# RWKV time mixing on one core: numerators in two PSUM banks with one output operation, state matmuls in the denominators' banks, and every second v cast by GpSimd

## The chip, the core and the metric

The kernel runs on one core of a Trainium2 chip. A core has five engines, each with its own stream of instructions that it starts in order: TensorE (PE; its weight loads are listed as PEld), VectorE (DVE), ScalarE (ACT), GpSimd (POOL) and SyncE (SP). [...] The metric is device microseconds of one execution.

## The reference

Batch 16, 2048 time steps, 256 channels, float32. Channels and batches are independent, and time is a recurrence:

```
for b in range(batch):
    aa, bb, pp = 0, 0, -1e38
    for t in range(seq_len):
        kk, vv = k[b, t], v[b, t]
        ww = u + kk;  qq = max(pp, ww);  e1, e2 = exp(pp - qq), exp(ww - qq)
        output[b, t] = (e1 * aa + e2 * vv) / (e1 * bb + e2 + 1e-08)
        ww = pp - w + kk;  qq = max(ww, kk);  e1, e2 = exp(ww - qq), exp(kk - qq)
        aa, bb, pp = e1 * aa + e2 * vv, e1 * bb + e2, qq
```

So an output is a weighted sum of v over the past, divided by the sum of the weights. aa and bb are the two running sums, and pp is their scale.

## The kernel before

**Tiles.** Time is cut into 16 chunks of 128 steps, and each chunk into two halves of 64. A unit n = 4c + p is chunk c of four batches: 128 time steps on the partitions by 4 x 256 values (512 KB of k, 512 KB of v, 512 KB of output). There are 64 units. The text calls one pass of the main loop, line 342, a slot; slot n starts unit n, and an output follows nine or ten slots later.

**What one unit goes through.** `round_k` (L161) copies k to a matmul type. `logs` (L170, L174) makes the logarithms of two sets of weights, E and Z, in a four-bank PSUM tile X: triangular matrices times k, plus multiples of w and u. `exps` (L178, ACT) takes exponentials into EZR, a ring of 12 units with four parts: E, Z, E·v and Z·v. `times_v` (L196) writes the last two, from a bfloat16 copy of v. Nine slots later `den` (L296) sums E and Z into two PSUM banks, and `recip` (L302, L303) takes the reciprocal on ACT as a logarithm and an exponential. Ten slots later `num` (L309) sums E·v and Z·v for one half of the columns (i = 0 or 1) into one bank, `mult` (L316) multiplies by the reciprocal, both run again for the other half, and `store` (L321) writes the unit.

**PSUM.** Eight banks: X has four, `den` two, `num` one, and "misc" one, which the three state tiles tot, TS and CT share. Each pool has a single buffer, so a producer waits until the last reader of the tile before it has finished.

**v.** The even units, and those below 8, come as float32 and are cast by DVE (`cast_v`, L191). The odd ones from 9 on are cast on their way in by the transfer (L70).

**The state.** E and E·v sum only within a half. What comes in from earlier halves is carried by a small chain per chunk: `sums` (L218, 16 narrow matmuls), `copy_sums` (L225), `turn` (L232, 4 transposing float32 matmuls), `state_logs` (L237, ACT), `state_offsets` (L243 to L250, 7 DVE operations), `state_weights` (L254, ACT, tile G), `state_chain` (L261 to L268, 6 DVE operations, ending in CB), `turn_back` (L275), and `inject` (L280, L285). The last copies the result to cb, and four transfers on SP's queue put it in the last row of each half of E and E·v of the chunk's own four units. `den` and `num` then sum it with the rest, so `den(4c)` in slot 4c + 9 must wait for these transfers.

**What sets the order.** Every instruction is kept in program order, so the main loop is the order. In a slot it is: loads of unit n + 6, `exps(n)`, the state work named "pe0", "act" and "dve0", `num(n - 10)` first half, `den(n - 9)`, `recip`, `mult` first half, `num` second half, `logs(n + 1)`, `round_k(n + 2)`, `mult` second half, `store`, `times_v(n)`, `cast_v(n + 1)`, and the state work "pe" and "dve". The state work of chunk c is spread over four slots, which the text calls A to D:

```
slot          state work of chunk c, before
A  n = 4c+4   sums and copy_sums at the end
B  n = 4c+5   turn ahead of num; state_logs; state_offsets at the end
C  n = 4c+6   state_weights ahead of recip; state_chain at the end
D  n = 4c+7   turn_back and inject at the start
```

All large transfers (k, v and the outputs) are issued from POOL's queue, in program order with POOL's own work; those of `inject` are issued from SP.

Of the kernel before, what the change touches and what calls it, by code (L numbers as in the profile page):

```python
# [7 lines left out]
F32 = mybir.dt.float32  # L8
F32R = mybir.dt.float32r
BF16 = mybir.dt.bfloat16  # L10
ALU = mybir.AluOpType
ACT = mybir.ActivationFunctionType
# [3 lines left out]
def kernel(  # L16
# [9 lines left out]
    K = tc.keep_in_program_order  # L26
    PE, DVE, SC, POOL, SP = nc.tensor, nc.vector, nc.scalar, nc.gpsimd, nc.sync

    B, T, Dm = k.shape
    HS = 64  # L30
# [18 lines left out]
    psx = ctx.enter_context(tc.tile_pool(name="psx", bufs=1, space=bass.MemoryType.PSUM))  # L49
    psd = ctx.enter_context(tc.tile_pool(name="psd", bufs=1, space=bass.MemoryType.PSUM))  # L50
    psn = ctx.enter_context(tc.tile_pool(name="psn", bufs=1, space=bass.MemoryType.PSUM))
    psm = ctx.enter_context(tc.tile_pool(name="psm", bufs=1, space=bass.MemoryType.PSUM))

    K(SC.preload_act_table_set("natural_log_exp_and_others"))

# [1 line left out]
    kr_of, vr_of, VB = {}, {}, {}  # L57

    def v_mode(n):
        return "dve" if n < 8 or n % 2 == 0 else "dma"  # L60

    def load(n, kq=None, vq=None):
        c, p = divmod(n, 4)
# [29 lines left out]
    def select(ap, cmp, fill, base, cm, pattern):  # L93
        K(POOL.affine_select(out=ap, in_=ap, pattern=pattern, compare_op=cmp,
                             fill=fill, base=base, channel_multiplier=cm))
# [4 lines left out]
    def fill(ap, value):  # L100
        K(DVE.memset(ap.bitcast(F32) if ap.dtype == F32R else ap, value))
# [1 line left out]
    select(M1, GE, 0.0, -1, -1, [[1, 128]])  # L103
    select(I1, NE, 1.0, 0, -1, [[1, 128]])
    COf = matrix("COf", F32)
    for h in range(2):
        K(POOL.iota(COf[HS * h:HS * h + HS, :], pattern=[[0, 2], [1, HS]], base=-HS // 2 - h, channel_multiplier=0,
                    allow_small_or_imprecise_dtypes=True))
    for g in (2, 3):
        select(COf, NE, 1.0, -32 * g - 1, 1, [[0, 128]])  # L110
# [15 lines left out]
    mats = {}  # L126

    def sum_matrices():
        OH = consts.tile([128, 40], BF16, tag="OH", name="OH")
        fill(OH, 0.0)  # L130
        for h in range(2):
            fill(OH[HS * h:HS * h + HS, 8 + h:9 + h], 1.0)
            fill(OH[HS * h:HS * h + 1, 16 + h:17 + h], 1.0)
        Sel = consts.tile([128, 3, 2, 4, 2], F32, tag="Sel", name="Sel")
        fill(Sel, 0.0)
        for j, r in ((0, 64), (1, 0), (2, 8)):
            select(Sel[:, j], NE, 1.0, -r, 1, [[-1, 2], [-2, 4], [-32, 2]])
        mats["OH"], mats["Sel"] = OH, Sel.rearrange("p a h c i -> p (a h) (c i)")

    def out_matrices():  # L140
        Lx = matrix("Lx", F32)
# [14 lines left out]
    def ez(n):  # L156
        return EZR[:, :, n % RING]

    def round_k(n):
        km = consts.tile([128, 4, Dm], F32R, tag=f"km{n % 2}", name="km") if n < 2 else KM[n - 2]  # L160
        K(DVE.tensor_copy(km, kr_of.pop(n)))  # L161
        KM[n] = km
# [37 lines left out]
    LL = consts.tile([128, 2, 2 * NST + 2, 32], F32, tag="LL", name="LL")  # L200
    A_of = [consts.tile([128, 8, 32], F32, tag=f"A{j}", name=f"A{j}") for j in range(2)]
    AB_of = [consts.tile([128, 2, 2, 32], F32, tag=f"AB{j}", name=f"AB{j}") for j in range(2)]

    CB_of = [consts.tile([128, 4, 128], BF16, tag=f"CB{j}", name=f"CB{j}") for j in range(2)]

    def state_start():
# [4 lines left out]
        K(DVE.memset(AB_of[0][:, :, 0, :], 0.0))  # L211

    def sums(c):
        t = psm.tile([128, D], F32, tag="misc", name="tot")
        for p in range(4):
            for j in range(4):
                q, i = divmod(j, 2)
                K(PE.matmul(t[32 * j:32 * j + 32, :], mats["OH"][:, 8 - 2 * p:40 - 2 * p],  # L218
                            ez(4 * c + p)[:, 2 * q, i, :], start=p == 0, stop=p == 3,
                            tile_position=(0, 32 * j), skip_group_check=True))  # L220
        st[c, "tot"] = t

    def copy_sums(c):
        ts = tiny.tile([128, D], F32, tag="ts", name="ts")
        K(DVE.tensor_copy(ts, st.pop((c, "tot"))))  # L225
        st[c, "ts"] = ts

    def turn(c):
        TS = psm.tile([128, 6, 4, 8], F32, tag="misc", name="TS")
        ts = st.pop((c, "ts"))  # L230
        for b in range(4):
            K(PE.matmul(TS[:, :, b, :], ts[:, 128 * b:128 * b + 128], mats["Sel"], start=True, stop=True,  # L232
                        skip_group_check=True))
        st[c, "TS"] = TS.rearrange("p a b m -> p a (b m)")

    def state_logs(c):
        K(SC.activation(LL[:, :, 2 * c + 2:2 * c + 4, :],  # L237
                        st[c, "TS"][:, 2:6, :].rearrange("p (a h) x -> p a h x", a=2), ACT.Ln))

    def state_offsets(c):  # L240
        A, last = A_of[c % 2], A_of[(c + 1) % 2]
# [13 lines left out]
        st[c, "G"] = G  # L255

    def state_chain(c):
        G, TS = st.pop((c, "G")), st.pop((c, "TS"))
        AB, nxt = AB_of[c % 2], AB_of[(c + 1) % 2]
        tb = tiny.tile([128, 2, 2, 32], F32, tag="tb", name="tb")  # L260
        K(DVE.tensor_mul(tb, TS[:, 0:4, :].rearrange("p (a h) x -> p a h x", a=2),  # L261
                         G[:, 4:6, :].unsqueeze(1).broadcast_to([128, 2, 2, 32])))
        for h in range(2):
            x = tiny.tile([128, 2, 32], F32, tag="x", name="x")
            K(DVE.tensor_mul(x, AB[:, :, h, :], G[:, h, :].unsqueeze(1).broadcast_to([128, 2, 32])))
            K(DVE.tensor_add(AB[:, :, 1, :] if h == 0 else nxt[:, :, 0, :], x, tb[:, :, h, :]))
        CB = CB_of[c % 2]
        K(DVE.tensor_mul(bass.AP(tensor=CB.tensor, offset=CB.offset, ap=[list(CB.ap[0]), [64, 2], [32, 2], [129, 4], [4, 8]]),  # L268
                         AB.rearrange("p a h (b m) -> p a h b m", b=4),
                         G[:, 2:4, :].rearrange("p h (b m) -> p h b m", b=4).unsqueeze(1).broadcast_to([128, 2, 2, 4, 8])))  # L270

    def turn_back(c):
        CT = psm.tile([128, 128], F32, tag="misc", name="CT")
        for b in range(4):
            K(PE.matmul(CT, CB_of[c % 2][:, b, :], mats["Id"], start=b == 0, stop=b == 3, skip_group_check=True))  # L275
        st[c, "CT"] = CT

    def inject(c):
        cb = small.tile([128, 128], BF16, tag="cb", name="cb")
        K(DVE.tensor_copy(cb, st.pop((c, "CT"))))  # L280
        r0 = 4 * c % RING
        for q in range(2):
            for h in range(2):
                r, x = HS * h + HS - 1, 32 * (2 * q + h)
                K(SP.dma_start(  # L285
                    out=EZR[r:r + 1, 2 * (1 - q), r0:r0 + 4, :, :].rearrange("o p i (b x) -> o (p i b) x", b=4),
                    in_=cb[x:x + 32, :]))
# [15 lines left out]
        K(SC.activation(rd, rd, ACT.Exp, scale=-1.0))  # L303
        RD[n] = rd

    def num(n, i):
        d = psn.tile([128, D], F32, tag="num", name="num")
        for m, q in (("LN", 2), ("IdN", 3)):
            K(PE.matmul(d, mats[m], ez(n)[:, q, i, :], start=q == 2, stop=q == 3, skip_group_check=True))  # L309
        NUM[n, i] = d  # L310

    def mult(n, i):
        if i == 0:
            OT[n] = opool.tile([128, 4, Dm], F32, tag="ot", name="ot")
        o = OT[n].rearrange("p (i n) d -> p i (n d)", i=2)
        K(DVE.tensor_mul(o[:, i, :], NUM.pop((n, i)), RD[n][:, i, :]))  # L316

    def store(n):
        RD.pop(n)
        c, p = divmod(n, 4)  # L320
        K(POOL.dma_start(out=out[4 * p:4 * p + 4, c * TC:(c + 1) * TC, :].rearrange("n t d -> t n d"),  # L321
                         in_=OT.pop(n)))

    later = {}
    for c in range(NST):
        s = 4 * c + 3
        for slot, where, f in ((s + 1, "pe", sums), (s + 1, "dve", copy_sums),
                               (s + 2, "pe0", turn), (s + 2, "act", state_logs), (s + 2, "dve", state_offsets),
                               (s + 3, "act", state_weights), (s + 3, "dve", state_chain),
                               (s + 4, "pe0", turn_back), (s + 4, "dve0", inject)):  # L330
            later.setdefault((slot, where), []).append((f, c))

    def small_work(n, where):
        for f, c in later.pop((n, where), []):
            f(c)
# [6 lines left out]
    for n in range(NP + LAG + 2):  # L342
        q, qp = n - LAG, n - LAG - 1
        live, out_q, out_qp = n < NP, 0 <= q < NP, 0 <= qp < NP
        if n + AHEAD < NP:
            load(n + AHEAD)
        if live:
            exps(n)
        small_work(n, "pe0")
        small_work(n, "act")  # L350
        small_work(n, "dve0")
        if out_qp:
            num(qp, 0)
        if out_q:
            den(q)
            recip(q)
        if out_qp:
            mult(qp, 0)
            num(qp, 1)
        if n + 1 < NP:  # L360
            logs(n + 1)
        if n + 2 < NP:
            round_k(n + 2)
        if out_qp:
            mult(qp, 1)
            store(qp)
        if live:
            times_v(n)
        if n + 1 < NP:
            cast_v(n + 1)  # L370
        if n == 1:
            sum_matrices()
        if n == 3:
            out_matrices()
        small_work(n, "pe")
        small_work(n, "dve")
    assert not later


# [29 lines left out]
```

## Time and profile before

| what | value |
|---|---|
| three runs | 400.68, 403.47, 408.91 us; median 403.47 |
| profiled execution | 401.16 us, of it a span of 399.2 us from the first to the last instruction |
| busy time | PE 286.8, DVE 283.7, ACT 260.6, POOL 158.9 us |
| mean granted TensorE clock | 0.923 |
| moved by transfers | 94.15 MB, mean 236 GB/s |

The profile is of one execution. Its page gives the busy time of each engine, the span in 40 slices, the chain of work that ended last, and groups of instructions by line. Each group has its busy time, the mean of one instruction in ns, and the time that its engine sat idle before it. The trace behind it answers further questions: who waited for whom, the instructions in order of time, or the busy times in a stretch. The starts of `exps` (L178) mark the slots: those of units 12, 24, 25, 26, 27, 28, 60 and 63 are at 77.93, 144.70, 148.49, 154.62, 159.84, 165.46, 339.12 and 354.10 us. In the profile, "clock" is the TensorE clock that was granted, as a share of the full one.

### The profile page before, as it was taken

The page shows a single profiled execution, that of the slowest core. Times are in us where ns is not written, and L with a number is a line of the kernel's source. Part 1 is how long each engine was busy: PE and PEld are TensorE (multiplying, and loading weights), DVE is VectorE, ACT ScalarE, POOL GpSimd, SP SyncE. Part 2 cuts the span into 40 slices and gives each one's busy share as a digit, 9 for nine tenths or more (in the row PEclk, how much of TensorE's full clock was granted, in tenths as well). Part 3 has the DMA queues.
Part 4 walks back from the last instruction along what each step waited for, and adds up shares of the span by engine and source line. Part 5 has one row for each costly group of instructions (what it writes and reads, how often), then busy time and mean ns, then how long its engine had stood idle before and what let it go on. Part 6 is the DMA issues. An engine that isn't in the chain of part 4 may idle for free.

```text
span 399.2 us, 4440 instructions
## 1 busy us (share of the span) xinstructions
PE 286.8 (72%) x1449; PEld 133.9 (34%) x1472; DVE 283.7 (71%) x559; ACT 260.6 (65%) x225; POOL 158.9 (40%) x203
## 2 busy tenths in 40 slices
PE   0345769787868697777789686869777778957672
PEld 0122334343424334333334242433433333423220
DVE  1266665877787877878777878787787977776542
ACT  1134344975777877877758777777787775876472
POOL 7134322452545453535435454545353531012131
PEclk9999857996999889999969999988999996999896
DMA  7978975699899989999989899997999991333344
GB/s 245 349 248 193 316 202 136 174 284 257 264 254 296 273 204 282 261 279 281 287 237 287 264 295 250 302 275 208 280 262 286 268 285 56 105 109 138 122 165 158
DMA packets 43062, 94.15 MB, mean 236 GB/s; under 512 B 6160, under 2 KB 22560, under 8 KB 43040
## 3 DMA queue, kind: packets, MB, share of 16 engines
q0 software_dynamic: 37824, 91.24, 78.2%
q1 hardware_dynamic: 4144, 1.59, 1.7%
q10 hardware_dynamic: 1072, 1.06, 0.9%
q8 instruction: 11, 0.18, 0.2%
q14 instruction: 11, 0.09, 0.1%
HBM read 67.13 MB, written 33.55 MB: 252 GB/s over the span
## 4 chain that ended last, share of the span: by engine, by line
PE 34%; DVE 29%; issue 21%; DMA 7%; ACT 4%; POOL 3%; POOLq 0%; DVEq 0%
DVE EZR L196 10%; PE num L309 10%; PE X L174 7%; DVE ot L316 7%; PE den L296 6%; DMA kr<-in_k_dram 4%; PE tot L218 3%; ACT EZR L178 3%; PE TS L232 3%; POOL out_dram L321 3%; DVE vb L191 3%; PE X L170 3%; DVE ts L225 2%; DMA out_dram<-ot 1%; DMA vr<-in_v_dram 1%
## 5 line engine op out<-in xcount | busy, mean ns | idle before, releaser
L178 ACT ACTIVATE EZR<-X 128x2048 bf16<-128x2048 f32 x64 | 120.0, 1875 | 51.7 <-PE X L174 51.4
L321 POOL DMA_DIRECT2D out_dram<-ot x64 | 48.9, 763 | 196.5 <-DVE ot L316 192.6
L316 DVE TENSOR_TENSOR ot<-num,rd 128x512 f32<-128x512 f32 x128 | 88.3, 690 | 53.7 <-PE num L309 44.5
L302 ACT ACTIVATE rd<-den 128x1024 f32<-128x1024 f32 x64 | 65.2, 1019 | 51.3 <-PE den L296 51.3
L196 DVE TENSOR_TENSOR EZR<-EZR,vb 128x2048 bf16<-128x2048 bf16 x64 | 77.8, 1216 | 5.4 <-ACT EZR L178 5.3
L309 PE MATMUL num<-EZR,LN 128*128 128x512 bf16 x121 | 49.0, 405 | 35.2 <-DVE ot L316 34.6
L303 ACT ACTIVATE rd<-rd 128x1024 f32<-128x1024 f32 x64 | 67.9, 1061 | 2.0
L66 POOL DMA_DIRECT2D kr<-in_k_dram x62 | 55.7, 899 | 16.9 <-DVE km L161 14.8
L170 PE MATMUL X<-WU,CO 1*128 1x512 f32 (+1 forms) x256 | 36.1, 554 | 27.9 <-ACT EZR L178 15.1
L174 PE MATMUL X<-km,NLE 128*128 128x512 f32 x128 | 51.9, 489 | 3.3 <-DVE km L161 3.3
L161 DVE CAST km<-kr 128x1024 fp32r<-128x1024 f32 x64 | 44.0, 688 | 8.6 <-DMA kr<-in_k_dram 6.1
L309 PE MATMUL num<-EZR,IdN 128*128 128x512 bf16 x114 | 46.3, 406 | 0.4
L174 PE MATMUL X<-km,NLZ 128*128 128x512 f32 x128 | 45.5, 440 | 0.0
L296 PE MATMUL den<-EZR,Id 128*128 128x512 bf16 x128 | 40.9, 403 | 0.1
L296 PE MATMUL den<-EZR,L 128*128 128x512 bf16 x126 | 40.4, 403 | 0.7
L170 PEld LDWEIGHTS X<-WU,CO 1*128 1x128 f32 (+1 forms) x256 | 13.5, 202 | 58.3 <-ACT EZR L178 26.5
L74 POOL DMA_DIRECT2D vr<-in_v_dram x34 | 31.0, 912 | 2.4 <-DVE vb L191 2.4
L309 PEld LDWEIGHTS <-IdN 128*128 128x128 bf16 x128 | 13.1, 102 | 54.7 <-issue 54.7
L174 PEld LDWEIGHTS X<-km,NLZ 128*128 128x128 f32 x128 | 27.0, 211 | 6.9
L174 PEld LDWEIGHTS X<-km,NLE 128*128 128x128 f32 x128 | 21.0, 207 | 21.5 <-issue 17.2
L232 PE MATMUL TS<-Sel,ts 128*128 128x48 f32 x128 | 17.4, 279 | 12.9 <-DVE ts L225 12.9
L275 PE MATMUL CT<-Id,CB 128*128 128x128 bf16 x64 | 7.6, 254 | 25.8 <-DVE CB L268 25.8
(53 smaller groups left out, 214.2 us busy)
## 6 DMA issues: line engine op xcount, KB each, us to landing
out_dram<-ot POOLq DMA_DIRECT2D x64, 512.0 KB, 4.1
kr<-in_k_dram POOLq DMA_DIRECT2D x62, 512.0 KB, 6.2
vr<-in_v_dram POOLq DMA_DIRECT2D x34, 512.0 KB, 6.6
vb<-in_v_dram POOLq DMA_DIRECT2D x28, 256.0 KB, 7.2
kr<-in_k_dram SPq DMA_DIRECT2D x2, 512.0 KB, 14.3
vr<-in_v_dram ACTq DMA_DIRECT2D x2, 512.0 KB, 5.7
EZR<-cb SPq DMA_DIRECT2D x64, 8.0 KB, 4.8
wuf<-in_w_dram SPq DMA_DIRECT2D x4, 2.0 KB
```

What stands on the lines that cost most here:

```text
L66: K((kq or POOL).dma_start(out=kr, in_=src[0]))
L161: K(DVE.tensor_copy(km, kr_of.pop(n)))
L170: K(PE.matmul(X[:, q, i, :], CO[g:g + 1 + q, :], WU[g:g + 1 + q, :], start=True, stop=False, tile_position=(g, 0), skip_group_check=True))
L174: K(PE.matmul(X[:, q, i, :], m, km[:, i, :], start=False, stop=True, skip_group_check=True))
L178: K(SC.activation(ez(n)[:, 0:2], X_of.pop(n), ACT.Exp))
L196: K(DVE.tensor_mul(ez(n)[:, 2:4], ez(n)[:, 0:2], vb.unsqueeze(1).broadcast_to([128, 2, 2, D])))
L296: K(PE.matmul(d[:, i, :], mats[m], ez(n)[:, q, i, :], start=q == 0, stop=q == 1, skip_group_check=True))
L302: K(SC.activation(rd, DEN.pop(n), ACT.Ln, scale=RS))
L303: K(SC.activation(rd, rd, ACT.Exp, scale=-1.0))
L309: K(PE.matmul(d, mats[m], ez(n)[:, q, i, :], start=q == 2, stop=q == 3, skip_group_check=True))
L316: K(DVE.tensor_mul(o[:, i, :], NUM.pop((n, i)), RD[n][:, i, :]))
L321: K(POOL.dma_start(out=out[4 * p:4 * p + 4, c * TC:(c + 1) * TC, :].rearrange("n t d -> t n d"), in_=OT.pop(n)))
```

## The change

- `num` makes both halves of the columns at once, in a tile of two banks; `mult` is one 128x1024 operation.
- The "misc" bank is given up for that. tot, TS and CT are now made in `den`'s tile: they wait until `recip` has read the denominators of their slot, and the `den` after them waits until DVE has copied them out.
- `sums` makes 32 matmuls of 256 columns in place of 16 of 512, so tot has 256 columns. `turn` makes 2 matmuls in place of 4, with 96 columns in place of 48. TS is copied to SBUF by a new DVE operation, `copy_turned` (192 columns), which `state_logs` and `state_chain` then read.
- `state_chain` writes CB as its fourth operation, ahead of the two that only the next chunk needs.
- State work moves in the slots (the last part of the diff): `turn` and `turn_back` now come behind `logs`, `state_offsets` and `state_weights` into slot C, `state_chain` to the start of slot D, `inject` to the end of slot D.
- In a slot `den` now precedes `num`, and `cast_v(n + 1)` precedes `mult` and `times_v(n)`.
- All v come as float32, and POOL casts the odd units from 9 on.

```diff
     def v_mode(n):
-        return "dve" if n < 8 or n % 2 == 0 else "dma"
+        return "pool" if n >= 8 and n % 2 else "dve"
...
     def sums(c):
-        t = psm.tile([128, D], F32, tag="misc", name="tot")
+        t = psd.tile([128, 2, D], F32, tag="den", name="tot")
         for p in range(4):
-            for j in range(4):
-                q, i = divmod(j, 2)
-                K(PE.matmul(t[32 * j:32 * j + 32, :], mats["OH"][:, 8 - 2 * p:40 - 2 * p],
-                            ez(4 * c + p)[:, 2 * q, i, :], start=p == 0, stop=p == 3,
-                            tile_position=(0, 32 * j), skip_group_check=True))
+            for o in range(2):
+                x = 24 - 16 * o - 2 * p
+                for j in range(4):
+                    q, i = divmod(j, 2)
+                    K(PE.matmul(t[32 * j:32 * j + 32, 0, 0:Dm], mats["OH"][:, x:x + 32],
+                                ez(4 * c + p)[:, 2 * q, i, Dm * o:Dm * o + Dm],
+                                start=p == 0 and o == 0, stop=p == 3 and o == 1,
+                                tile_position=(0, 32 * j), skip_group_check=True))
...
+    def copy_turned(c):
+        T6 = small.tile([128, 6, 32], F32, tag="T6", name="T6")
+        K(DVE.tensor_copy(T6.rearrange("p a x -> p (a x)"), st.pop((c, "TS"))[:, 0, 0:192]))
+        st[c, "T6"] = T6
...
-    def num(n, i):
-        d = psn.tile([128, D], F32, tag="num", name="num")
+    def num(n):
+        d = psn.tile([128, 2, D], F32, tag="num", name="num")
         for m, q in (("LN", 2), ("IdN", 3)):
-            K(PE.matmul(d, mats[m], ez(n)[:, q, i, :], start=q == 2, stop=q == 3, skip_group_check=True))
-        NUM[n, i] = d
+            for i in range(2):
+                K(PE.matmul(d[:, i, :], mats[m], ez(n)[:, q, i, :], start=q == 2, stop=q == 3,
+                            skip_group_check=True))
+        NUM[n] = d
...
-        K(DVE.tensor_mul(o[:, i, :], NUM.pop((n, i)), RD[n][:, i, :]))
+        K(DVE.tensor_mul(OT[n].rearrange("p (i n) d -> p i (n d)", i=2), NUM.pop(n), RD.pop(n)))
...
-        for slot, where, f in ((s + 1, "pe", sums), (s + 1, "dve", copy_sums),
-                               (s + 2, "pe0", turn), (s + 2, "act", state_logs), (s + 2, "dve", state_offsets),
-                               (s + 3, "act", state_weights), (s + 3, "dve", state_chain),
-                               (s + 4, "pe0", turn_back), (s + 4, "dve0", inject)):
+        for slot, where, f in ((s + 1, "pe", sums), (s + 1, "last", copy_sums),
+                               (s + 2, "pe", turn), (s + 2, "last", copy_turned),
+                               (s + 3, "act", state_logs), (s + 3, "dve", state_offsets),
+                               (s + 3, "act2", state_weights),
+                               (s + 4, "dve0", state_chain), (s + 4, "pe", turn_back),
+                               (s + 4, "last", inject)):
```

The loop's order after the change, with s = 4c + 3 above: `exps`, "act", "dve0", `den`, `recip`, `num`, `logs`, `round_k`, `cast_v`, `mult`, `store`, "dve", `times_v`, "act2", "pe", "last".

## The prediction

> **What bounds the kernel now.** The page's busy times first: no engine is full.
>
> ```profile
> PE 286.8 (72%) x1449; PEld 133.9 (34%) x1472; DVE 283.7 (71%) x559; ACT 260.6 (65%) x225; POOL 158.9 (40%) x203
> ...
> PE 34%; DVE 29%; issue 21%; DMA 7%; ACT 4%; POOL 3%; POOLq 0%; DVEq 0%
> ```
>
> The chain that ended last passes between PE and DVE: hand-overs set the time. Next the busy times by chunk, cut at the start of each slot B (us; PE, PEld, DVE, ACT, POOL busy; clock; DMA share; GB/s):
>
> ```profile
> 148.49:169.30 20.81, 15.97 (x94) 7.66 (x92) 17.05 (x34) 16.21 (x15) 10.00 (x12) 1.00 0.97 276
> 169.30:190.32 21.02, 16.26 (x95) 7.73 (x96) 17.25 (x34) 16.23 (x16) 10.19 (x13) 1.00 0.97 277
> 190.32:213.30 22.98, 18.70 (x98) 8.43 (x100) 17.43 (x34) 16.18 (x15) 10.39 (x14) 0.85 0.90 255
> ```
>
> A chunk takes 20.9 at full clock, and about every third one 23.0, with the clock at half for 7 us. Units 12 to 60 are 12 chunks in 261.2, 21.8 each. Then the timeline of one chunk, for what ends each wait:
>
> ```profile
> 161.61 0.40 PE L275 MATMUL CT<-Id,CB 128*128 128x128 bf16 x4 [1.81 <-DVE CB L268]
> 162.04 0.29 DVE L280 CAST cb<-CT 128x128 bf16<-128x128 f32 x1 [0.49 <-PE CT L275]
> 162.37 2.40 SPq L285 DMA_DIRECT2D EZR<-cb  x4
> ...
> 165.46 1.88 ACT L178 ACTIVATE EZR<-X 128x2048 bf16<-128x2048 f32 x1
> ...
> 169.30 1.88 ACT L178 ACTIVATE EZR<-X 128x2048 bf16<-128x2048 f32 x1
> ...
> 170.30 0.69 DVE L225 COPY ts<-tot 128x512 f32<-128x512 f32 x1 [0.73 <-PE tot L218]
> ...
> 171.04 1.09 PE L232 MATMUL TS<-Sel,ts 128*128 128x48 f32 x8 [0.80 <-DVE ts L225]
> ...
> 172.66 0.69 DVE L316 TENSOR_TENSOR ot<-num,rd 128x512 f32<-128x512 f32 x1 [1.67 <-PE num L309]
> ...
> 175.60 1.88 ACT L178 ACTIVATE EZR<-X 128x2048 bf16<-128x2048 f32 x1
> ```
>
> Slot A (165.46) takes 3.84: ACT's own work (exps 1.77, Ln 1.05, Exp 1.02). Slots B, C, D take 6.30, 5.25 and 5.6, since state work stands ahead of `num` on PE. Two more answers matter below. The instructions of L285, the inject transfers, give their time to landing:
>
> ```profile
> DMA to landing us min/median/max: 1.8/4.8/5.9
> ```
>
> And the timeline, with the clock by microsecond, shows where the clock falls:
>
> ```profile
> 134.89 0.38 PE L309 MATMUL num<-EZR,LN 128*128 128x512 bf16 x1 [1.77 <-DVE ot L316]
> ```
>
> ```profile
> 138.00:139.00 1.00, 0.14 (x2) 0.15 (x3) 0.76 (x3) 1.00 (x1) 0.76 (x2) 0.50 1.00 373
> ```
>
> Behind a PE gap of 1.77 us it is at half from about 136.75 to 143.6, and that slot lasts 7.3 in place of 5.6.
>
> **The change, added up.** I follow the four queues round one chunk after the change. A step is from one start to the next, from this trace: `den` 0.86, its end seen by ACT 1.06 after its start; X 1.62; km and cast 0.60; times_v 1.13; a semaphore 0.05. A `mult` of 1024 columns is extrapolated from 690 ns at 512 and 220 ns at 64 (L265): 1.23, a step of 1.14, 0.08 less than two halves. `num` lets `mult` start 1.05 after it. tot's copy of 256 columns is 0.42 and T6's of 192 is 0.36, between L225 (691 ns, 512) and L280 (291 ns, 128).
>
> 1. DVE alone, from `mult` in slot C to cb at the end of D: mult 1.14, seven offsets 1.40, times_v 1.13, chain 1.45 (the row's 1.5), km 0.60, cast 0.60, mult 1.14, times_v 1.13, cb 0.29 = 8.9. The offsets now stand behind `mult`, and G waits for them; behind G on ACT is the next `exps`, behind that X. Slot C gets longer (6.1), slot D falls to ACT's 3.9.
> 2. `den` of slot A now waits for cb, as CT lies in its banks. Semaphore and den 0.92, num 0.86, X until sums 1.51, sums 1.10, tot's copy 0.42 = 4.8.
> 3. The next `den` waits for that copy: 0.92, num 1.05, mult 1.14, times_v 1.13, T6 0.36 = 4.6. TS (at most the row's 1.09, I take 0.65) runs beside mult and times_v.
> 4. `den` of slot C waits for T6: 0.92, num 1.05 = 2.0.
>
> Together 20.3 against 20.9 at full clock: two banks and shorter state work buy 0.6, and the three copies that `den` waits for take the rest back. Two things come on top.
>
> **Inject.** cb came early in slot D and now ends it, and `den(4c)` needs the third and fourth transfer. Before it started 10 us after cb; by step 2 it wants to 4.9 after. The four issues take 2.40, the fourth starts 1.84 after the first, and lands at the row's median 4.8 later: 6.7. So PE waits 1.8, with X and the next `exps` queued behind. From below, a landing of 1.8 (an idle tail) makes 3.6 and no wait; from above, 5.9 and 0.6 more for an issue make 8.3, a wait of 3.4. I take the median, since the store and loads of slot D are still issued just ahead of cb. Chunk: 22.1.
>
> **Clock.** PE's gaps become about 1.8 and 2.0 in slot D, and 1.8 at the inject wait; before they were 1.70 and 1.75, and one chunk in three lost 2.1. More chunks will. But half clock in slot A stretches the very den, num and X that run beside the transfers: 20.3 + 2.1 = 22.4, hardly more than 22.1. I take 22.3 as the mean.
>
> [...]
>
> **At nothing, with the cover.**
> - sums: 16 matmuls of 512 took 1.05, the array's rate for four column strips. 32 of 256 have the same columns, from 0 more to one issue each at the old pace, 32 x 0.053 = 1.7, so 0.85 more. The inject wait covers 1.8 of it; without that wait I count 0.3.
> - POOL's cast, 128x1024: POOL's nearest rows are 241 ns at 16 columns and 293 at 128, a line that gives 0.7, and 342 ns at 128 eight times is 2.7. I take 1.3. It runs after the store (0.76) and two loads (0.75 each, 1.12 to 1.21 beside a DVE cast), some 2.7 after a `mult`, while DVE waits for `num`. Only above 1.8 does it meet the offsets. Behind it on POOL stands the store alone, which waits for a later `mult`; the odd v now take float32 buffers that a cast freed a slot before. POOL has 10 of 21 us busy, and SP's queue holds nothing but the injects.
> - DMA: 5 to 25 us moved 344 GB/s of float32 loads at a share of 1.05, so 1.6 us a load; the tail's stores (149 GB/s at 0.43) cost 1.5. Four units cost 18.8 a chunk. Before the share was 0.97 x 20.9 = 20.3, so a casting load cost over 2: the traffic eases. At 22 it binds nothing, at 18.8 it would.
>
> [...]
>
> **Ends.** To unit 12 before: 77.9. Slot 5 took 5.44 against 4.77 around it, since turn stood ahead of X: 0.7 less, 77.2. From unit 64's slot (some 359.9) to the end: 39.3. The last plain slots took 2.89 each (377.08 to 391.54 in five). After, num 1.05, mult 1.23 and a semaphore make 2.33: 2.8 less. Slots 64 to 68 took 17, by the steps above 14: 33.5.
>
> **Sum.** 77.2 + 13 x 22.3 + 33.5 = 400.6 of span; the profiled execution has 2.0 around it: 402.6, say 403. Against its own 401.16 that is 0.4% more; the median shown is 403.47, 2.3 above the profiled run.
>
> **Rivals.**
> - *Faster.* The injects land within 5 us of cb, with the queues eased, and the clock falls no oftener: 20.3 + 0.3 + 0.7 = 21.3, so 77.2 + 276.9 + 33.5 + 2.0 = 390. For it: landings of 1.8 in the idle tail. Against: 4.4 to 5.9 wherever all three streams ran.
> - *Slower by the clock.* The gaps at cb and at the inject wait each halve it, at places where nothing covers: 22.1 + 2.1 = 24.2, 427. It decides where the lost clock falls in slots B and C, behind the inject wait. For it: three gaps of 1.8 in a chunk. Against: a stretched slot A closes the third.
> - *Slower by POOL.* The cast takes 2.7, as eight affine selects would, and the offsets wait 0.9 in each chunk: 22.3 + 0.9 = 23.2, 414. For it: affine selects are POOL's only like rows. Against: the line through the other two.
> - *The change does not do what it says.* The four state tiles could stay in the way as before; but `turn` and `turn_back` do come behind X in program order, so that is excluded, and the cost is only in the copies.
>
> **Chances.** No change, at 403, 0.42, with its own range 396 to 411 (21.8 to 22.9 a chunk). The faster rival 0.22. Slower by the clock 0.18, by POOL 0.10, both in part 0.08. A measurement of this kernel tells about 2% from no change (its runs spread by 2%), which is 395 to 411.5. So faster 0.22, same 0.42, slower 0.36. For 8 in 10 the range takes in most of the faster case and stops short of the full clock loss: 387 to 424.
>
> **What would show it.** Slots A, B, C, D near 5.5, 6.6, 6.1 and 3.9. `den` in slot B waiting on an EZR transfer for 1 to 2 us; if it waits only on ts, step 2 was the limit and the faster rival holds. G (L262) starting right behind the last offset, and exps right behind G. `mult` near 1.23 x 64, T6 0.36, POOL's cast 0.7 to 1.8 with no DVE wait on it. Chunks of 24 with clock below 0.85 would speak for the clock. Wrong would be above all a chunk below 20.3, which would mean that the queues overlap in a way that the steps don't have.

## The result, and the profile after

The changed kernel takes 432.37 us (median of four runs, 431.75 to 439.18), the kernel before 402.14 (four runs, 400.68 to 408.91). The ratio is 1.074, with a 95% interval of 1.067 to 1.081. The forecast was 403, within 387 to 424: the kernel is slower, and beyond the range. The profiled execution has a span of 429.7.

The page's busy times, and its row of the granted clock in 40 slices of the span:

```profile
PE 302.8 (70%) x1634; PEld 147.5 (34%) x1664; DVE 284.5 (66%) x511; ACT 259.5 (60%) x225; POOL 185.8 (43%) x234
...
PEclk9999666697988959696878969696877889596888
```

DVE and ACT do as much as before, POOL 27 us more (the casts), and PE 16 us more, though its work hardly grew: its matmuls ran longer (one of `num` took 631 ns at 201 us, where the clock is at half, and 379 at 209, where it is full), and the clock is below 9 in 26 of the 40 slices, where it was in 12 before. The same chunks by windows, now cut where slot A starts; columns as before:

```profile
149.67:173.78 24.11, 18.78 (x103) 9.28 (x104) 17.39 (x31) 16.07 (x16) 11.86 (x14) 0.78 0.84 267
173.78:196.99 23.21, 17.29 (x105) 8.39 (x105) 17.59 (x31) 16.08 (x16) 12.20 (x14) 0.86 0.85 273
196.99:221.52 24.53, 18.76 (x102) 9.22 (x104) 17.38 (x31) 16.06 (x15) 11.86 (x14) 0.78 0.80 258
```

Not every third chunk is disturbed but every one, at a clock of 0.78 to 0.86 (0.78 to 0.87 over the twelve from unit 12 to 60). DMA is less busy than before (share 0.80 to 0.85, where it was 0.90 to 0.97). The timeline from the end of slot D into slot B; L284 is `turn_back`, L290 and L295 are `inject`, L306 is `den`:

```profile
195.12 0.50 PE L170 MATMUL X<-WU,CO 1*128 1x512 f32 x4 [1.64 <-ACT EZR L178]
...
196.58 0.40 PE L284 MATMUL CT<-Id,CB 128*128 128x128 bf16 x4
196.99 1.86 ACT L178 ACTIVATE EZR<-X 128x2048 bf16<-128x2048 f32 x1
...
198.81 0.28 DVE L290 CAST cb<-CT 128x128 bf16<-128x128 f32 x1
199.12 2.87 SPq L295 DMA_DIRECT2D EZR<-cb  x4
199.14 0.58 PE L306 MATMUL den<-EZR,L 128*128 128x512 bf16 x1 [2.16 <-DVE cb L290]
...
205.48 1.88 ACT L178 ACTIVATE EZR<-X 128x2048 bf16<-128x2048 f32 x1 [2.32 <-PE X L174]
207.32 0.42 DVE L227 COPY ts<-tot 128x256 f32<-128x256 f32 x1 [2.16 <-PE tot L219]
208.19 0.59 PE L306 MATMUL den<-EZR,L 128*128 128x512 bf16 x2 [0.92 <-DMA EZR<-cb]
```

PE is idle for 1.64 us ahead of X, and after 1.9 us of work for 2.16 more, until cb has been copied out of `den`'s banks. The clock by microsecond shows what follows (us, then the five engines, clock, DMA share, GB/s; the rows between 199 and 207 are left out, all at 0.50):

```profile
197.00:198.00 1.00, 0.00 (x0) 0.00 (x0) 1.00 (x2) 1.00 (x2) 0.00 (x0) 0.63 0.89 336
198.00:199.00 1.00, 0.00 (x0) 0.00 (x0) 1.00 (x2) 0.84 (x1) 0.95 (x2) 0.50 0.70 258
...
207.00:208.00 1.00, 0.27 (x8) 0.00 (x0) 0.68 (x2) 0.36 (x1) 0.00 (x0) 0.75 0.74 132
```

From 197.26 to 207.50 it is at half: 10.2 us, all of slot A but its first 0.3 and the first 2 us of slot B, though PE is busy nearly throughout from 200 to 207. Slot A lasts 8.49 here. Behind it, in slot B, `den` still waits 0.92 for the inject transfers, 9.1 after cb.

Two things about the clock are easily missed. First, the 35 times at which it changes in this trace, from 47.08 to 425.96, lie whole multiples of 3.41 us apart, and so do the 15 in the kernel before, from 47.78 to 392.52: here it falls at 197.26, rises at 207.50, falls at 221.16 and rises at 227.99, which is three, four and two such intervals. Each chunk loses the clock for two or three of them, 6.8 or 10.2 us. Second, it fell 0.28 into the gap of 2.16, so that most of that gap came too late to call it. The interval that ended with the fall is this window:

```profile
193.85:197.26 3.41, 1.86 (x12) 1.15 (x13) 3.31 (x10) 3.38 (x4) 0.19 (x1) 1.00 0.99 322
```

PE was busy for 1.86 of 3.41, a share of 0.55. From unit 12 to 60 that share is 0.52 to 0.55 in each of the 12 intervals that end with a fall, and 0.61 or more in the 43 others at full clock. In the kernel before the share does not part them: five intervals of 0.48 to 0.54 ended with a fall, and four of 0.48 to 0.53 did not.

The inject transfers' time to landing, and the two kinds of wait of `den` in the whole span (us, times, longest):

```profile
DMA to landing us min/median/max: 2.1/5.5/6.8
```

```profile
PE den L306 <- DVE cb L290: 27.7, 15, 2.2
PE den L306 <- DMA EZR<-cb: 14.6, 9, 2.7
```

The span is 30.5 longer than before. Units 12 to 60 take 285.4, 23.78 a chunk, where they took 261.2: 24.2 of it. After unit 60 follow 65.4 (before 60.1), and ahead of unit 12 are 78.9 (77.9).

### The profile page after: what moved, and what is told of

It reads as the page before. It is cut to its first block, busy times and chain, and to the rows that moved or that the text cites. A ratio compares the mean times of both kernels' runs of the same rounds, so it can differ in the third digit from the quotient of the medians.

```text
span 429.7 us, 4779 instructions
## 1 busy us (share of the span) xinstructions
PE 302.8 (70%) x1634; PEld 147.5 (34%) x1664; DVE 284.5 (66%) x511; ACT 259.5 (60%) x225; POOL 185.8 (43%) x234
## 3 DMA queue, kind: packets, MB, share of 16 engines
q10 hardware_dynamic: 1072, 1.06, 0.8%
## 5 line engine op out<-in xcount | busy, mean ns | idle before, releaser
L326 DVE TENSOR_TENSOR ot<-num,rd 128x1024 f32<-128x1024 f32 x64 | 78.3, 1223 | 85.1 <-ACT rd L312 50.0
L312 ACT ACTIVATE rd<-den 128x1024 f32<-128x1024 f32 x64 | 65.4, 1022 | 68.8 <-PE den L306 45.4
L306 PE MATMUL den<-EZR,L 128*128 128x512 bf16 x113 | 39.2, 419 | 58.9 <-DVE cb L290 27.7
L161 DVE CAST km<-kr 128x1024 fp32r<-128x1024 f32 x64 | 57.4, 898 | 6.7 <-DMA kr<-in_k_dram 4.2
L65 POOL DMA_DIRECT2D kr<-in_k_dram x62 | 52.0, 839 | 10.5 <-DVE km L161 8.3
L73 POOL DMA_DIRECT2D vr<-in_v_dram x62 | 48.5, 782 | 18.6 <-DVE vb L191 17.2
L174 PE MATMUL X<-km,NLE 128*128 128x512 f32 x128 | 54.8, 515 | 1.4 <-DVE km L161 1.4
L174 PE MATMUL X<-km,NLZ 128*128 128x512 f32 x128 | 48.3, 464 | 0.0
L320 PE MATMUL num<-EZR,LN 128*128 128x512 bf16 x127 | 44.7, 438 | 2.8 <-DVE ot L326 1.9
L306 PE MATMUL den<-EZR,Id 128*128 128x512 bf16 x114 | 43.1, 456 | 3.0 <-issue 2.9
L306 PEld LDWEIGHTS <-L 128*128 128x128 bf16 x128 | 11.6, 105 | 74.5 <-issue 57.1
L189 POOL CAST vb<-vr 128x1024 bf16<-128x1024 f32 x28 | 33.3, 1190 | 0.0
L191 DVE CAST vb<-vr 128x1024 bf16<-128x1024 f32 x36 | 26.5, 736 | 0.9 <-DMA vr<-in_v_dram 0.9
```

The costliest lines, as they stand in the source:

```text
L65: K((kq or POOL).dma_start(out=kr, in_=src[0]))
L174: K(PE.matmul(X[:, q, i, :], m, km[:, i, :], start=False, stop=True, skip_group_check=True))
L306: K(PE.matmul(d[:, i, :], mats[m], ez(n)[:, q, i, :], start=q == 0, stop=q == 1, skip_group_check=True))
L312: K(SC.activation(rd, DEN.pop(n), ACT.Ln, scale=RS))
L320: K(PE.matmul(d[:, i, :], mats[m], ez(n)[:, q, i, :], start=q == 2, stop=q == 3, skip_group_check=True))
L326: K(DVE.tensor_mul(OT[n].rearrange("p (i n) d -> p i (n d)", i=2), NUM.pop(n), RD.pop(n)))
```

## The experiments

The theory from these lines: two things late in each chunk lie side by side. One is the half clock that comes with PE's gaps around X and CT; the other is that `den(4c)` needs transfers which start only at the end of slot D. The rivals are POOL's cast, one of the two alone, and the issue of the 32 small matmuls of `sums`. The last falls by the trace: they took 1.06 us at full clock (lag10_ctfill), where 16 of twice the size took 1.05, and 1.9 at half.

The times beside the runs of the kernel before on the same chip (medians 403 to 405), and from each trace the clock and the mean chunk from unit 12 to 60 with its slots. Where the ratio is left out, the executions spread too widely to give one, and the slots of fill_swap and fill_den are those of executions of 422.68 and 438.86, longer than their medians:

| kernel | us (lowest to highest) | ratio to before, 95% | clock | chunk | A | B | C | D |
|---|---|---|---|---|---|---|---|---|
| before | 402.14 (400.68 to 408.91) | | 0.923 | 21.77 | 3.82 | 6.25 | 5.39 | 6.31 |
| the change | 432.37 (431.75 to 439.18) | 1.067 to 1.081 | 0.829 | 23.78 | 7.88 | 6.00 | 6.08 | 3.82 |
| lag10 | 423.74 (422.65 to 427.51) | 1.044 to 1.058 | 0.840 | 23.54 | 8.08 | 5.61 | 6.08 | 3.78 |
| fill | 457.91 (455.91 to 463.10) | 1.126 to 1.139 | 0.862 | 26.24 | 5.76 | 10.14 | 6.57 | 3.77 |
| lag10_fill | 381.07 (380.14 to 382.35) | 0.940 to 0.950 | 0.993 | 20.44 | 5.62 | 4.96 | 6.08 | 3.77 |
| lag10_ctfill | 382.70 (382.53, 382.86) | 0.936 to 0.956 | 0.985 | 20.46 | 5.65 | 4.97 | 6.07 | 3.77 |
| fill_ab | 437.17 (433.58, 440.75) | | 0.982 | 23.84 | 5.65 | 8.33 | 6.08 | 3.77 |
| fill_swap | 419.29 (415.90, 422.68) | | 0.936 | 23.43 | 5.76 | 7.71 | 6.19 | 3.77 |
| fill_den | 434.37 (423.37 to 441.72) | | 0.958 | 24.76 | 5.66 | 9.12 | 6.22 | 3.77 |
| dma_cast | 430.41 (429.49 to 432.65) | 1.061 to 1.072 | 0.816 | 23.87 | 8.21 | 5.81 | 6.08 | 3.77 |
| lag10_fill_dma | 382.24 (380.67 to 383.65) | 0.941 to 0.956 | 0.982 | 20.48 | 5.65 | 4.97 | 6.08 | 3.77 |
| before_fill | 390.86 (389.47 to 392.73) | 0.962 to 0.981 | 0.995 | 21.00 | 3.82 | 6.29 | 5.24 | 5.64 |
| before_pool | 428.53 (424.99 to 433.85) | 1.046 to 1.067 | 0.868 | 23.51 | 4.11 | 6.23 | 5.14 | 8.03 |
| before_pool_ahead | 432.28 (431.28 to 432.38) | 1.064 to 1.083 | 0.894 | 24.00 | 3.78 | 6.66 | 8.12 | 5.44 |
| early_lag10 | 391.75 (390.74 to 391.89) | 0.961 to 0.974 | 0.887 | 21.29 | 6.15 | 5.28 | 6.08 | 3.77 |
| early_fill | 367.12 (364.67 to 370.01) | 0.897 to 0.914 | 0.989 | 19.59 | 4.50 | 5.25 | 6.07 | 3.77 |

"Idle matmuls" below multiply an identity by an old unit's E into a place that the next matmuls overwrite or that nobody reads. They leave the outputs as they are and only keep PE at work while it would wait.

### lag10: the transfers get a slot more

```diff
-    LAG = 9
+    LAG = 10
```

> After the change, with denominators ten and numerators eleven slots after their unit (LAG 10), so that den(4c) has one more slot before it needs the inject transfers; one more slot at the end costs 2.4. Side by side (my theory: in slots A and B the half clock and the inject transfers run beside each other, and each hides most of the other): den in slot B no longer waits for a transfer, the 0.8 to 1.7 of it in over half of the chunks go, half clock stays: 13 x 0.7 less, 2.4 more, about 426. Clock alone: the transfers never bound, 435. Inject alone: the chunk falls from 23.8 to 20.5, about 392.

`den` never waits for a transfer in slot B any more, yet slot A is still at half clock (8.08) and the chunk gains 0.24 only. Between the two profiled executions (spans of 429.7 and 423.0), 5.9 are gained ahead of unit 12 and 2.9 in the chunks, and 2.0 lost behind unit 60. So the transfers alone are not the cause.

### fill: no long gap on PE in slots D and A

```diff
+        # ahead of CT's four matmuls, in CT's second bank
+        for i in range(7):
+            K(PE.matmul(t[:, 1, :], mats["Id"], ez(4 * c + 3)[:, 1, i % 2, :], start=True, stop=True, ...))
...
+        # ahead of num in slot D, in num's banks
+            for i in range(8):
+                K(PE.matmul(d[:, i % 2, :], mats["Id"], ez(n)[:, 1, i % 2, :], start=True, stop=True, ...))
```

> After the change, with idle matmuls whose results are overwritten or never read: 7 of 512 columns ahead of the four of CT, 8 ahead of num in slot D, so that PE has no gap over 1.5 us there. The clock should stay at full in slot A. Side by side: then den in slot B waits for the injects, which landed 7.7 to 9.1 after cb, and the chunk is 15.4 + 8 = 23.4: 427 and a clock above 0.93. Clock alone: 2.9 less in each chunk, 395. Inject alone: no change, 432.

A clear miss: 25.5 us slower. Slot A is at full clock, 5.76, as meant. But `den` in slot B now stands before transfers that have not landed:

```profile
214.60 1.86 ACT L178 ACTIVATE EZR<-X 128x2048 bf16<-128x2048 f32 x1
...
220.25 1.88 ACT L178 ACTIVATE EZR<-X 128x2048 bf16<-128x2048 f32 x1 [0.30 <-PE X L174]
224.47 0.59 PE L309 MATMUL den<-EZR,L 128*128 128x512 bf16 x1 [3.27 <-DMA EZR<-cb]
229.36 1.88 ACT L178 ACTIVATE EZR<-X 128x2048 bf16<-128x2048 f32 x1 [0.87 <-PE X L174]
```

Slot A is 5.65 (214.60 to 220.25) and slot B 9.11. `den` waits 3.27, and over that gap the clock falls, so that the next matmuls run at half: two of `num` take 1.06 here, 0.59 in slot A, and in most chunks those of X are slower too (two take 1.22 in place of 0.73). Slot A's half clock had been hiding most of this wait.

### lag10_fill: both

The edits of lag10 and fill together.

> Both edits, the later denominators and the idle matmuls. Side by side: neither is left, the chunk is the 20.3 of the steps, 13 x 3.4 less than 432 and 2.4 more: about 391, far more than the two edits alone add up to. Clock alone: as the idle matmuls alone, and 2.4. Inject alone: as LAG 10 alone.

```profile
174.40:194.86 20.46, 18.32 (x119) 9.42 (x119) 16.86 (x31) 16.08 (x16) 11.66 (x14) 1.00 0.93 308
```

One edit brings 8.6, the other costs 25.5, both together bring 51.3 (432.37 to 381.07), ten more than expected. Of the profiled span 40 are gained in the twelve chunks, 6.6 ahead of them and 5.2 behind. The two delays are largely parallel: without the waits for transfers the chunk is still 23.54, and without the half clock in slot A it is 26.24, since the late `den` then calls a half clock of its own in slot B. Without both the chunk is 20.44.

### lag10_ctfill: idle matmuls behind X alone

lag10 with the seven idle matmuls ahead of CT alone.

> LAG 10 and only the 7 idle matmuls ahead of CT. If the gap behind CT alone calls the half clock: 381 and a clock of 0.99 as with all idle matmuls. If the gap of 1.6 ahead of X does it too in some chunks, as gaps of 1.77 did in one chunk of three before: 388 to 400.

The chunk is 20.46. The wait ahead of X stays (1.62), the gap behind CT shrinks to 0.64, and the clock holds: work in this one place is enough. That does not make the length of the gap behind CT the cause: in early_lag10 below it is 1.02, and the clock still falls. The intervals of 3.41 here have PE busy for 0.59 or more of them, above the 0.52 to 0.55 at the falls of the change. But a chunk of 20.46 is almost six intervals (20.48), so they cut each chunk of this run at the same place; whether the clock would hold with the wait of 1.62 at another place is not shown.

### fill_ab, fill_swap, fill_den: the price of the transfers

fill_ab adds 14 idle matmuls behind `sums` in tot's second bank; fill_swap issues E·v's two transfers ahead of E's; fill_den puts ten idle matmuls into `den`'s banks ahead of `den(4c)`. All three include fill.

```diff
+        for i in range(14):                       # fill_ab, at the end of sums
+            K(PE.matmul(t[:, 1, :], mats["Id"], ez(4 * c + 3)[:, 1, i % 2, :], start=True, stop=True, ...))
...
-        for q in range(2):                        # fill_swap, in inject
+        for q in (1, 0):
...
+        if n % 4 == 0 and 8 <= n + LAG < NP:      # fill_den, in den
+            for i in range(10):
+                K(PE.matmul(d[:, i % 2, :], mats["Id"], ez(n)[:, 1, i % 2, :], start=True, stop=True, ...))
```

> After the change, with the idle matmuls of the run before and 14 more behind sums, in the bank of tot's tile that is not used, so that PE has work while den in slot B waits for the injects. LAG is 9 as in the change, so the inject wait stays and only the clock is cured. My theory after the first four runs: the inject wait by itself costs 3 a chunk at full clock (den starts 7.7 or more after cb, the chunk is 15.4 + 8 = 23.4), and the rest of the 458 is the half clock that this wait calls in slot B: 420 to 430, clock above 0.95. Rival: idle matmuls themselves slow the transfers or the chain: 450 or more.

The clock holds (0.982), but tot's copy waits for the idle matmuls too, and `den` comes when they end, 8.1 to 8.2 after cb in ten of the twelve chunks: they set slot B's 8.33 themselves. The run tells only that a `den` so late gives the time of the change at full clock as well.

> After the change, with the idle matmuls in slot D, and the four inject transfers issued in the other order, so that den waits for the first and second in place of the third and fourth. If what makes them late is the issue on SP's queue (2.6 to 3.0 for four), den starts 1.2 to 1.5 earlier in each chunk: 458 less 16 to 20, 440. If they land together once the bulk traffic ahead of them is through, the order changes nothing: 458.

From cb to `den` it took 5.0 to 8.2 (mean 6.6), against 7.0 to 8.5 in fill (7.8). That is 1.2 earlier, about two issues of 0.6, as the first of the two cases had it; the scatter is too wide to call the issue shown. The time fell by 39, twice what was expected, as five of the twelve chunks kept the clock at 1.00 (none in fill).

> The changed kernel with the idle matmuls of fill and ten more ahead of den of unit 4c (slot B), 2.1 us at full clock, written where den then writes; outputs unchanged. If the inject wait by itself costs 2.8 a chunk (7.9 from cb to den in fill, against 5.0 where nothing has to land): slot B 7.8, chunk 23.2, 12 chunks 279, with 80 ahead and 60 behind 419, and 2 around it, about 420, at a clock above 0.95. If the prediction's 1.8 were right, the idle matmuls themselves would set slot B at 7.1: chunk 22.5, 412. If the clock still halves in B, 440 or more.

The transfers landed later than in fill, so that `den` came 7.4 to 10.0 after cb, and the runs scatter from 423 to 442. Nine of the twelve chunks kept the clock, and took 22.90 to 24.83. Two of them (windows of one chunk each):

```profile
230.94:255.03 24.09, 20.88 (x131) 10.33 (x129) 17.61 (x31) 16.09 (x15) 11.95 (x14) 1.00 0.81 266
255.03:278.34 23.31, 20.91 (x131) 10.33 (x129) 17.60 (x31) 16.07 (x15) 11.97 (x14) 1.00 0.82 272
```

At a clock of 1.00 they took 24.09 and 23.31, with `den` 8.6 and 7.8 after cb. The nine lie 2.5 to 4.4 above lag10_fill's 20.44: that is the wait for the transfers by itself, 1.8 in the forecast. In the two shortest `den` came only 0.1 behind the idle matmuls, which bound them from below. The expected 420 was missed by 14: the landing varies more than I assumed, and three chunks lost the clock (27.4 to 28.0).

### dma_cast and lag10_fill_dma: the odd v cast by the transfer again

```diff
-        return "pool" if n >= 8 and n % 2 else "dve"
+        return "dve" if n < 8 or n % 2 == 0 else "dma"
```

The cast v lie in buffers of their own, and v's pool has four buffers in place of six.

> After the change, but the odd v from 9 on are cast by their transfer as before, in buffers of their own. If POOL's cast costs nothing on the path (side by side, and both others): 432, within 1%. If it is part of the loss, by a longer DVE cast beside it (km took 1.73 in place of 0.68 in slot C): up to 1.0 a chunk, 419.

> The changed kernel with LAG 10 and the idle matmuls, but odd v cast by the transfer. With clock and injects out of the way, this prices POOL's cast. If it is hidden: 381 within 1%. If the km cast beside it (1.74 in place of 0.69) costs on the path: up to 1 a chunk less, 368. If casting transfers load the DMA (20.3 a chunk by the sum on record against a chunk of 20.5): 385 to 390.

430.41 against 432.37, and 382.24 against 381.07: no cost of the cast shows in the change, at either clock. It takes 1.19 in the mean, and `mult` and the offsets do not wait for it. One operation is stretched beside POOL, `round_k`. Of the change's own timeline, first POOL's rows and then DVE's:

```profile
188.63 0.75 POOL L73 DMA_DIRECT2D vr<-in_v_dram  x1
189.37 1.41 POOL L189 CAST vb<-vr 128x1024 bf16<-128x1024 f32 x1
```

```profile
188.16 1.73 DVE L161 CAST km<-kr 128x1024 fp32r<-128x1024 f32 x1
190.28 1.23 DVE L326 TENSOR_TENSOR ot<-num,rd 128x1024 f32<-128x1024 f32 x1 [0.38 <-issue]
```

It takes 1.73 in place of 0.68, but `mult` behind it starts only when `num` is ready, 0.38 after km's end: slot C, where this is, has that room.

### before_fill: does the kernel before lose to the clock too?

Five idle matmuls ahead of `den` in slot C and five ahead of CT in slot D of the kernel before.

> The kernel before the change, with idle matmuls in its two PE gaps: 5 ahead of den in slot C and 5 ahead of CT's in slot D. If the clock is what the before kernel loses too, its chunks all take 20.9 to 21.2 in place of 21.8: 393 to 397, and the 381 of the changed kernel with both cures shows what the change itself brings at full clock (0.4 to 0.6 a chunk, and 6 at the end). If the gaps are not what halves its clock: 402 or more.

390.86, chunk 21.00: the forecast's 20.9 at full clock. The kernel before loses 11 to 14 us to half clock (402.14 above, 404.96 beside this run). With both at full clock, the change (lag10_fill) is ahead by 9.8 us: 0.56 in each chunk, and the rest at the two ends, where LAG 10 has its part too.

### before_pool and before_pool_ahead: the cast alone, in the order of before

```diff
-        return "dve" if n < 8 or n % 2 == 0 else "dma"
+        return "pool" if n >= 8 and n % 2 else "dve"
...
+        if n + 1 < NP and v_mode(n + 1) == "pool":    # before_pool_ahead alone: ahead of the first mult
+            cast_v(n + 1)                             # and of the store, in place of behind them
```

> The kernel before with only the odd v loaded as float32 and cast by POOL: this part of the change alone. Hidden cast: 403, the same. If the longer km cast beside it (1.74) meets the chain: up to 1 a chunk, 416. If the lighter DMA traffic helps: 395.

428.53: a miss by far, and slot D is 8.03 where it was 6.31. There the cast runs behind the store, and meets `state_chain`. In its timeline, L189 is the cast, L265 makes the chain's two products, and L275 is CT:

```profile
190.75 1.05 POOL L189 CAST vb<-vr 128x1024 bf16<-128x1024 f32 x1
...
190.95 0.94 DVE L265 TENSOR_TENSOR x<-AB,G 128x64 f32<-128x64 f32 x1
...
192.18 0.22 DVE L265 TENSOR_TENSOR x<-AB,G 128x64 f32<-128x64 f32 x1
...
193.07 0.40 PE L275 MATMUL CT<-Id,CB 128*128 128x128 bf16 x4 [2.53 <-DVE CB L268]
```

The first of two equal products ends only with the cast, 0.72 late. So PE's gap ahead of CT grows from 1.81 to 2.53, and the clock is at half behind it in nearly every chunk (0.82 to 0.91 by chunk; one in the middle kept 1.00 and took 21.42).

> The kernel before with every second v cast by GpSimd, as in before_pool, but with the cast ahead of the first mult and of the store in program order, so that GpSimd casts right behind the two loads. If before_pool lost its time because the cast met state_chain (0.94 us for a product of 0.22, CT 0.7 later, half clock in slot D): the product back at 0.22, the gap ahead of CT back at 1.8, slot D 5.6 to 6.3, and 400 to 410. If GpSimd's cast costs by itself (its own time, float32 loads, or the wait of times_v for it): slot D stays at 8 and the time at 422 to 430.

432.28: half a miss. The product is back at 0.22 and slot D at 5.44, but the cast now meets `state_offsets` (L247), with `num` waiting behind, and once in each chunk a km (2.13 in place of 0.68):

```profile
188.69 1.76 DVE L247 SCALAR_TENSOR_TENSOR A<-LL,A 128x32 f32<-128x32 f32 x1
189.34 1.05 POOL L189 CAST vb<-vr 128x1024 bf16<-128x1024 f32 x1
...
191.92 0.59 PE L309 MATMUL num<-EZR,LN 128*128 128x512 bf16 x1 [3.21 <-DVE ot L316]
```

An offset takes 1.76 in place of 0.19, PE waits 3.21, and slot C (8.12) pays in place of slot D. So "the cast meets `state_chain`" was too narrow: an offset beside it is late as well, and in this order PE waits behind both. Not every DVE operation is: the `mult` at 190.28 above ran beside the end of a cast and took its 1.23.

Both late operations, of 0.94 and of 1.76, ended within 0.1 after the cast beside them.

### early_lag10 and early_fill: state work earlier in slot D

lag10 with `turn_back` right behind `logs` and `inject` ahead of `times_v`; early_fill has eight idle matmuls ahead of `num` in slot D and two ahead of CT besides.

```diff
-                               (s + 4, "dve0", state_chain), (s + 4, "pe", turn_back),
-                               (s + 4, "last", inject)):
+                               (s + 4, "dve0", state_chain), (s + 4, "pe0", turn_back),
+                               (s + 4, "dve", inject)):
...
             logs(n + 1)
+        small_work(n, "pe0")
```

> As the run before without any idle matmuls. With cb 1.1 earlier the PE gap behind CT shrinks from 2.1 to about 1.0, and the one ahead of X stays at 1.6. If the gap behind CT is what halves the clock in slot A, the clock is above 0.95 and the time near 370. If either gap of 1.6 does: 395 to 410 with a clock of 0.85 to 0.9.

> The changed kernel with LAG 10, cb copied ahead of times_v in slot D (inject moved from the end of the slot to just behind mult), 8 idle matmuls ahead of num in slot D and only 2 ahead of CT. By the steps on record the DVE run to cb loses one times_v of 1.13, so den in slot A starts 1.1 earlier in each chunk: 20.5 less 1.1 = 19.4, 13 x 1.1 = 14 less than the 381 with both cures: 367, faster than both kernels. Rival: another queue (ACT's 16 or the DMA's 18.8 a chunk, or times_v now late for the sums) takes the place: 375 or more.

```profile
191.34:210.94 19.60, 17.25 (x114) 8.95 (x114) 18.01 (x31) 16.07 (x15) 11.92 (x14) 1.00 0.93 317
```

With cb 1.1 earlier, `den` of slot A comes 1.1 earlier and slot A is 4.50; slot B gives 0.29 of it back. early_fill's 367.12 is what was expected and beats both kernels, 0.905 of before (0.897 to 0.914). Its chunk is no whole number of intervals of 3.41, so they cut it at changing places; the share of PE never falls below 0.74 between units 12 and 60, and the clock holds throughout.

Without idle matmuls the clock still halves in slot A (6.15), in every chunk but the first. The time, 391.75, is a little below the second case that was expected, not near the first: with the gap behind CT at 1.02 the clock falls all the same. The window that ends with a fall, `den` behind the gap, and the clock beside it:

```profile
195.41:198.82 3.41, 1.86 (x12) 1.15 (x13) 3.31 (x10) 3.38 (x4) 0.27 (x1) 1.00 1.02 321
```

```profile
199.51 0.58 PE L306 MATMUL den<-EZR,L 128*128 128x512 bf16 x1 [1.02 <-DVE cb L290]
```

```profile
199.00:200.00 1.00, 0.49 (x1) 0.21 (x2) 1.00 (x3) 1.00 (x1) 0.43 (x1) 0.50 0.77 299
```

PE is busy for the same 1.86 of 3.41 as in the change. So the gap behind CT need not be long: what the two falls have in common is how little PE does in the 3.41 before them, and most of its idle time there lies ahead of X. The half clock is shorter than in the change, though: one interval in eight of these chunks, three in the other three.

## Why the prediction was wrong, by its own steps

**Steps 1 to 4 were right.** At full clock they sum to 20.3; lag10_fill measures 20.44. Slot C was 6.1 (6.08 measured), slot D 3.9 (3.82), step 2 4.8 from cb to the copy's end (4.96 in lag10_fill), `mult` 1.23 (1.223), T6 0.36 (0.350). G starts behind the last offset and `exps` right behind G, as step 1 had it.

**At nothing.** The cast was rightly free here (dma_cast), and for the reason given: at 1.05 to 1.41 it ends before the offsets begin, and only a km with slack meets it. The *rival by POOL* falls for this kernel. That the same cast costs 24 to 29 us in the order of before shows how much of this hangs on the order of the change. There a product beside the cast took 0.94 in place of 0.22 (before_pool).

**The Inject term was mis-sized.** It put `den` 6.7 after cb, with a bound of 8.3. Measured are 7.6 to 9.1, and 7.4 to 10.0 in fill_den. Both parts grew: the four issues took 2.5 to 3.4 in place of 2.40, and the landing a median of 5.5 in place of 4.8. That they landed no faster here, with DMA less busy (0.80 to 0.85, before 0.90 to 0.97), was against my reason for the faster rival, which falls with it. The wait alone is worth 2.5 to 4.4, not 1.8.

**The Clock term failed.** It said that "half clock in slot A stretches the very den, num and X that run beside the transfers", so it was to cost 0.2 on top. The gap came as foreseen (2.0 forecast, 2.16 measured), but the clock halves in every chunk, for 6.8 or 10.2 us. Slot A goes from 5.65 to 7.88, and cb to the copy's end from 4.96 to between 6.7 and 8.7. The absorption itself is real: half clock alone costs 3.1 a chunk (lag10), the transfers alone 2.5 to 4.4 (fill_den), and side by side they make 3.3 (23.78 against 20.44). But both are larger than the forecast's 2.1 and 1.8, and in every chunk. The nearest rival was *slower by the clock* (427): its price was right, its place not. It asked for lost clock behind the inject wait in slot B; slot A alone was enough. Only in fill, fill_swap and fill_den does slot B lose it, as that rival said.

The forecast also took the length of a gap for what counts. Its own case speaks against that: in the kernel before the clock fell at 136.52, 1.6 after the gap of 1.77 had ended. From there on the falls lie 64.85 apart, which is 19 intervals of 3.41 and three chunks; in the change they lie 23.89 apart, seven intervals, one in each chunk. So that one chunk in three lost the clock before, and every one after, probably depends on where the intervals meet the gaps, which the forecast did not look at; no run changes that alone.

Short gaps were enough: the longest gap on PE in the twelve chunks of the change is 2.27, and idle matmuls behind X alone bring the clock back, from 0.840 in lag10 to 0.985 in lag10_ctfill.

**Ends.** The plain slots of the drain were right (2.33 forecast, 2.40 measured from 413.56 to 423.14). The "by the steps above 14" for slots 64 to 68 was wrong: they took 21.9 (388.5 to 410.4), at a clock of 0.73. There the state work runs with little beside it, PE has gaps of 1.2 to 2.5 around CT, and the clock is at half again from 388.41 to 395.24 and from 405.48 to 412.31. In sum against the forecast's span of 400.6: 1.7 more ahead of unit 12, 12 x 1.48 = 17.8 in the chunks, 1.9 in the chunk from unit 60, and 7.7 in the drain make 429.7.

**What stays open.** Why the transfers land later than before, and scatter from 7.4 to 10.0 after cb, was not settled. In early_fill, where they start 1.1 earlier in the slot, the median landing is 3.3; in lag10_fill it is 5.3, at nearly the same DMA share (0.93 to 0.96 and 0.93). So the share alone does not set it. Nor was it measured by itself how much PE has to do in an interval for the clock to hold: the share of busy time parts the intervals cleanly in the change (0.55 and 0.61), not in the kernel before.

## What to carry to other kernels

Price a new gap on PE by the clock too, and not by its own length alone: add up how busy PE is in the intervals at which the trace's clock changes, here 3.41 us. In the chunks from unit 12 to 60 of the kernel before and of the change it fell behind intervals with PE busy for 0.48 to 0.55 of them, though not behind each of those, and behind none of 0.61 or more; a few idle matmuls in one gap brought 41 us (lag10 to lag10_ctfill). When two delays end at the same instruction, removing one shows the other and can make things worse; test them alone and together before discarding either. Moving a small copy to the end of a slot moves every transfer and wait behind it, and GpSimd's cast beside DVE cost nothing here where the operation beside it had slack (km, 1.73 in place of 0.68), and 24 to 29 us where PE waited behind it (a product of 0.94 in place of 0.22, an offset of 1.76 in place of 0.19).

## What was not expected of the hardware

- The clock fell to half 0.28 us into a gap of 2.16, which followed 1.64 of idle and 1.9 of work, and fell as well with a gap of 1.02 in that place; half clock then lasted up to 10.2 us, though PE was busy from 200 on. It changed only at intervals of 3.41, and in the change it went with PE's busy share of the interval before: 0.52 to 0.55 ended with a fall, 0.61 and more did not.
- A DVE operation beside GpSimd's cast lasted far longer than by itself: 0.19 became 1.76 (before_pool_ahead), begun, by a profile that is rough on POOL, 0.65 before the cast and while GpSimd was issuing a load. km went from 0.68 to 1.73 in the change, and ended 0.9 before the cast beside it, not with it; this was not explained.
- The same small transfers landed in a median of 3.3 us in early_fill, 4.3 in fill, 5.5 in the change and 6.5 in fill_den, and the DMA share does not tell which: 0.93 to 0.96, 0.71 to 0.77, 0.80 to 0.85 and 0.69 to 0.82 in that order.
